# The state-space mixer of a two-layer transformer kernel: wave rows kept as three rows, all state products on GpSimd, deeper weight prefetch

## The chip, the cores and the metric

The kernel runs on one core of one Trainium2 chip, as one program. The metric is the device time of one execution in microseconds. The kernel before was run three times: median 3163.51 us, from 3159.57 to 3173.73. One further execution was recorded by the hardware profiler.

A core has engines that run side by side, each through its own list of instructions in order: TensorE (PE; its weight loads are listed apart as PEld), VectorE (DVE), ScalarE (ACT), GpSimd (POOL) and SyncE (SP, which here only issues transfers). They wait for one another through semaphores. A transfer is issued by SP, ScalarE or GpSimd into that engine's queue, and the transfers of one queue are issued in the order of the engine's list.

## The reference, cut to what matters

The model has two layers over 1024 latent tokens and 256 context tokens of width 1024. Layer 0 mixes tokens by attention and retention, layer 1 by a state-space mixer; each is followed by an MLP. The change lies in the mixer of layer 1:

```python
def s5_scan(u, a_bar, b_bar, c_mat, x0):      # complex, diagonal, 64 groups of 16 channels, 64 states each
        bu = jnp.einsum('btgh,gph->btgp', u_blk, b_bar)
        bu = bu.at[:, 0].add(a_bar * x)
        _, xs = lax.associative_scan(_affine_compose, (a, bu), axis=1)   # x_t = a_bar * x_{t-1} + bu_t
        y = jnp.einsum('btgp,ghp->btgh', xs, c_mat).real
...
    y_cf, x_cf = s5_scan(u_c, ab_f, bb_f, c_f, x0)                 # context first, forward
    y_cb, x_cb = s5_scan(u_c[:, ::-1], ab_b, bb_b, c_b, x0)        # and backward
    y_lf, _ = s5_scan(u_l, ab_f, bb_f, c_f, x_cf)
    y_lb, _ = s5_scan(u_l[:, ::-1], ab_b, bb_b, c_b, x_cb)
    y = y_lf + y_lb[:, ::-1] + d_skip * u
    z = gelu(y) @ w_glu;  out = z[:, :D] * sigmoid(z[:, D:])
```

## The kernel before, in words

**The mixer stage** is `s5_main`. The sequence is cut into chunks of 8 tokens: 160 columns, 32 of context and 128 of latents. Per group the chunk's inputs are multiplied into 64 complex states, the states are scanned over the 160 chunks, and the outputs come from the states plus a direct term inside the chunk (the matrix `T`). The complex decay is a real decay times a rotation. The rotation is taken out of the scan: the chunk inputs are multiplied by cosine and sine waves (rotated back), then a real scan runs, then the scanned states are rotated forward again by the same waves. So each step with a wave is four real products, and needs cosine, sine and negated sine.

The 64 groups are handled as 32 **pairs** `q` (two groups of 64 states fill the 128 partitions). For one pair:

- `load(q)`: SP issues the transfers of the pair's weights: `B` and `C` (256 KB each), the wave rows `CS` (320 KB, two rows from DRAM into rows 2 and 3 of a tile of four, three such tiles in rotation) and `T` in two parts. The loop calls it three pairs ahead.
- `spread(q)`, on ScalarE, called one pair ahead: L1493 writes the negated sine into row 0 of `CS`, L1494 copies the cosine into row 1, and L1497 writes the two decay rows `dec` of the scan (two `dec` tiles in rotation).
- `states(q)`: TensorE makes the chunk inputs (L1510) into two PSUM banks `b`, one per direction. VectorE multiplies each by the wave rows (L1516, `st`, twice: one 128x640 instruction per direction), adds the two halves (L1519, `sm`) and scans both directions in one instruction (L1521, `sz`). The forward rotation is one product per direction (L1527, `sy`, `e` in the code): on GpSimd, or on VectorE where `(2q+d) % 3` is zero, which is one product in two of every three pairs.
- `outs(q)`, called two pairs later: TensorE adds the direct term (L1539) and the states' outputs (L1545, 32 matmuls) into two banks `z` and `b` that stay open over four pairs; then four GELUs on ScalarE (L1550) write them to two of the 16 tiles `y`.

The inputs are read as `ut`, eight chunk positions by 16 channels on partitions. They are written to DRAM (`ud`) by the normalization that precedes the stage (`s5_in`: L1457 makes `us` on ScalarE, L1461 stores it) and read back by `inputs()`, L1472, eight transfers for eight groups, the first eight divided between ScalarE's and SP's queues.

**What sets the order.** The loop gives the program order and with it priorities; a tile scheduler orders each engine's instructions by these priorities and by what is ready in its own estimate. An engine then runs its list strictly in order. Buffers come from rotating pools: weights `B` and `C`, products `sy`, outputs `y` and many tiles of the stages around share 32 buffers of 128x512 (`atile`), and taking one waits until its former user is done. The 16 `y` tiles are taken when the stage starts.

**What follows** is the gated linear stage `glu`: it transposes `y` (L1586) and splits it into a high and a low part (`yh`, `yl`; L84). A side generator (`ada_rest`) computes modulation vectors for the last MLP: GpSimd issues broadcasts of a vector (`silr`, L201) and loads of weights (`aw`, L215), VectorE multiplies and reduces each (L219, called `ISA` in the order, `CUSTOM_DVE_ANT_0` in the trace). The scheduler mixes this work into the end of the mixer stage.

## Time and profile before

| | before |
|---|---|
| median of 3 runs | 3163.51 us (3159.57 to 3173.73) |
| profiled execution | 3176.57 us |
| its span, first to last instruction | 3174.8 us |
| mean granted TensorE clock | 0.965 of full speed |
| busy share of the span: PE, DVE, ACT, POOL | 93, 68, 39, 27 % |
| mixer stage, roughly | 2070 to 2240 us |
| busy in these 170 us: PE, DVE, ACT, POOL | 137.89, 147.46, 62.29, 70.39 us |

Times in the rows are microseconds unless marked ns. A row of the timeline has the start, the length, the engine, the line, the operation, the tile names as out<-in with the shape, the count, and in brackets the idle time just before it with what ended it. A row of the groups has the line, engine, operation and shapes, the count, then the busy time in all and the mean of one in ns, then the idle time of the engine just before these instructions and what ended most of it. A row of the windows has the stretch, its length, the busy time and count of PE, PEld, DVE, ACT and POOL, the granted clock, the busy share of the transfer engines and GB/s.

### The profile page before, as it was taken

To read this page: it belongs to the slowest core of one execution; us is meant where nothing else is said; L and a number is where in the kernel's file an instruction comes from. 1 tells how busy PE (TensorE), PEld (TensorE's weight loads), DVE (VectorE), ACT (ScalarE), POOL (GpSimd) and SP (SyncE) were. 2 spreads that over 40 slices of the span, in tenths; PEclk is the share of its full clock that TensorE was granted. 3 is DMA by queue.
4 is the path that set the end of the run, shared out by engine and by line. 5 is a ranking of instruction groups with operands and counts; after the bars stand their busy time and mean duration, and the time that the engine had idled before them with its cause. 6 is when DMAs were issued, how large, how long until landed. Compare 5 with 4: busy or idle time off the path is not lost. (4 is left out here: it accounts for less than half of the span.)

```text
span 3174.8 us, 45240 instructions
## 1 busy us (share of the span) xinstructions
PE 2967.9 (93%) x16683; PEld 2447.3 (77%) x16683; DVE 2143.4 (68%) x4088; ACT 1247.0 (39%) x2543; POOL 867.7 (27%) x936
## 2 busy tenths in 40 slices
PE   5899998899999999999998899878799999999998
PEld 3777777778878788888887777767578788888887
DVE  7776777777764588466676997488845555556555
ACT  6543322567672322333243367434234322222221
POOL 3642222355450131111113313133722111111111
PEclk8999998899999999999999999989899999999999
DMA  8132222210003252233329856498632111111111
GB/s 253 63 126 76 82 80 69 70 41 25 14 21 120 78 174 90 62 103 102 96 85 236 247 172 185 120 196 233 223 101 87 54 46 47 54 47 53 43 45 67
DMA packets 223774, 324.32 MB, mean 102 GB/s; under 512 B 52432, under 2 KB 147440, under 8 KB 223552
## 3 DMA queue, kind: packets, MB, share of 16 engines
q1 hardware_dynamic: 143376, 234.48, 25.0%
q0 software_dynamic: 20336, 49.70, 5.7%
q10 hardware_dynamic: 59840, 37.24, 3.9%
q8 instruction: 131, 2.15, 0.3%
q14 instruction: 91, 0.75, 0.1%
HBM read 267.96 MB, written 53.36 MB: 101 GB/s over the span
## 5 line engine op out<-in xcount | busy, mean ns | idle before, releaser
L84 POOL TENSOR_TENSOR al<-r,ah 128x512 fp32r<-128x512 f32 (+1 forms) x160 | 210.6, 1329 | 1258.2 <-ACT r L1064 1159.8
L1077 DVE SCALAR_TENSOR_TENSOR x<-b,mods,x 128x512 f32<-128x512 f32 (+1 forms) x483 | 460.5, 967 | 106.6 <-PE b L72 100.0
L84 DVE TENSOR_TENSOR ul<-mraw,uh 128x512 fp32r<-128x512 f32 x256 | 195.8, 770 | 387.3 <-ACT uh L76 386.7
L70 PE MATMUL b<-ah,dh 128*128 128x512 f32 (+1 forms) x1088 | 412.7, 380 | 3.5 <-ACT r L1060 1.5
L71 PE MATMUL b<-al,dh 128*128 128x512 f32 (+1 forms) x1088 | 411.1, 378 | 0.7 <-POOL al L84 0.7
L72 PE MATMUL b<-ah,dl 128*128 128x512 f32 (+1 forms) x1088 | 410.3, 378 | 0.0
L76 ACT ACTIVATE uh<-mraw 128x512 fp32r<-128x512 f32 x256 | 160.3, 628 | 466.9 <-PE b L71 255.9
L70 PE MATMUL b<-h2h,uh 128*128 128x512 f32 (+1 forms) x768 | 280.5, 365 | 28.2 <-DVE x L1077 22.1
L72 PE MATMUL b<-h2h,ul 128*128 128x512 f32 (+1 forms) x768 | 277.7, 362 | 6.2 <-DVE ul L84 6.2
L71 PE MATMUL b<-h2l,uh 128*128 128x512 f32 (+1 forms) x768 | 276.8, 360 | 0.0
L70 PEld LDWEIGHTS b<-ah,dh 128*128 128x128 f32 x1088 | 205.3, 189 | 42.7 <-issue 2.3
L72 PEld LDWEIGHTS b<-ah,dl 128*128 128x128 f32 x1088 | 205.3, 189 | 38.3
L71 PEld LDWEIGHTS b<-al,dh 128*128 128x128 f32 x1088 | 205.4, 189 | 38.2 <-POOL al L84 1.1
L76 ACT ACTIVATE dh<-mraw 128x512 fp32r<-128x512 f32 x192 | 116.0, 625 | 225.3 <-PE b L71 95.8
L70 PE MATMUL b<-h3h,uh 128*128 128x512 f32 x512 | 202.3, 396 | 0.0
L71 PE MATMUL b<-h3l,uh 128*128 128x512 f32 x512 | 200.1, 391 | 2.0 <-DVE h3l L316 1.8
L72 PE MATMUL b<-h3h,ul 128*128 128x512 f32 x512 | 201.2, 394 | 0.0
L84 POOL TENSOR_TENSOR pl<-pe,ph 128x512 fp32r<-128x512 f32 (+1 forms) x128 | 158.9, 1249 | 153.2 <-ACT ph L76 81.7
L70 PEld LDWEIGHTS b<-h2h,uh 128*128 128x128 f32 x768 | 146.3, 190 | 57.2 <-DVE x L1077 26.3
L1060 ACT ACTIVATE r<-b 128x512 f32<-128x512 f32 (+1 forms) x160 | 88.1, 551 | 239.6 <-PE b L72 184.9
L70 PE MATMUL z<-wh,hh 128*128 128x512 f32 (+1 forms) x400 | 161.1, 403 | 12.2 <-ACT scr L500 6.8
L72 PEld LDWEIGHTS b<-h2h,ul 128*128 128x128 f32 x768 | 146.7, 191 | 31.3 <-DVE ul L84 7.4
(426 smaller groups left out, 7195.0 us busy)
## 6 DMA issues: line engine op xcount, KB each, us to landing
mraw<-in_w SPq DMA_DIRECT2D x192, 512.0 KB
aw<-in_adat SPq DMA_DIRECT2D x64, 256.0 KB
mraw<-in_glu SPq DMA_DIRECT2D x32, 512.0 KB
aw<-in_adat POOLq DMA_DIRECT2D x48, 256.0 KB, 5.2
aw<-in_adat POOLq DMA_DIRECT2D x96, 128.0 KB, 3.6
CS<-csd SPq DMA_DIRECT2D x32, 320.0 KB
w<-in_adaw SPq DMA_DIRECT2D x32, 256.0 KB
wraw<-in_winr SPq DMA_DIRECT2D x32, 256.0 KB
```

The costliest lines, as they stand in the source:

```text
L70: mm(o, s[0], m[0], start=start, stop=False)
L71: mm(o, s[0], m[1], start=False, stop=False)
L72: mm(o, s[1], m[0], start=False, stop=stop)
L76: self.nc.scalar.activation(o, x, AF.Copy)
L84: e.tensor_tensor(o, x, h.bitcast(F32), ALU.subtract)
L1060: nc.scalar.activation(r[:, :n], b[:, :n], AF.Relu)
L1077: nc.vector.scalar_tensor_tensor(o, as_x(b), self.M[:, l, 5, oc, s:s + 1], xs, op0=ALU.mult, op1=ALU.add)
```

## The change

The wave tile holds three rows instead of four: sine and cosine come from DRAM (the two rows of `csd` swap places), and ScalarE writes only the negated sine behind them, one instruction per pair instead of two. The products read the three rows as two overlapping pairs: `turned` builds an access pattern that starts at the cosine row and steps one row up for one half of the result and one row down for the other. The wave tiles rotate over four instead of three and have their own loader `load_waves`, four pairs ahead. All products `sy` go to GpSimd. `B`, `C` and `T` are fetched up to six pairs ahead, fewer as the `y` tiles fill up, since a `y` tile is now taken when its four pairs are done. Of the stores of `us` for the last block of tokens, those of odd tiles move from SP's queue to GpSimd's, and the first eight loads of `ut` are divided between GpSimd and SP instead of ScalarE and SP.

```diff
@@ -1337,8 +1337,8 @@
                 nc.scalar.activation(t2(l), t2(l), AF.Sin, scale=-2.0 * math.pi, bias=self.hpi)
 
                 def store():
-                    nc.scalar.dma_start(self.csd[:, g0:g0 + n, 1], t3(q))
-                    nc.scalar.dma_start(self.csd[:, g0:g0 + n, 0], t3(l))
+                    nc.scalar.dma_start(self.csd[:, g0:g0 + n, 0], t3(q))
+                    nc.scalar.dma_start(self.csd[:, g0:g0 + n, 1], t3(l))
                 self.later(1, store)
             self.later(2, waves)
             yield
@@ -1458,7 +1458,7 @@
                                  AF.Identity, bias=sh)
             rows = self.ud[kt * P:(kt + 1) * P]
             for c0 in ((32 + t0 // 8,) if t0 < NL else (0, 160)):
-                (nc.sync if bi == 1 else nc.gpsimd).dma_start(rows[:, :, c0:c0 + nchunk], us.rearrange("p (s c) -> p s c", s=8))
+                (nc.sync if bi == 1 and kt % 2 == 0 else nc.gpsimd).dma_start(rows[:, :, c0:c0 + nchunk], us.rearrange("p (s c) -> p s c", s=8))
         return self.norm(1, 0, 1 if t0 >= NL else 0, lambda kt: x[:, kt, t0:t0 + n], n, o, tmp, b)
 
     def s5_main(self, p, last):
@@ -1471,27 +1471,36 @@
             for s in range(8):
                 engs[s % len(engs)].dma_start(ut[112 - 16 * s:128 - 16 * s, g0:g0 + n],
                                   self.ud[16 * g0:16 * (g0 + n), s].rearrange("(g q) c -> q g c", q=16))
-        self.Y = {(kt, th): self.atile(name="y") for kt in range(KT) for th in range(2)}
-        sl, A, ybank, decs = {}, {}, {}, {}
+        self.Y = {}
+        sl, A, ybank, decs, waves = {}, {}, {}, {}, {}
+
+        def load_waves(q):
+            waves[q] = p.tile([P, 2, 3, 160], F32, tag="CS", name="CS", bufs=4)
+            nc.sync.dma_start(waves[q][:, :, 0:2], self.csd[:, 2 * q:2 * q + 2])
 
         def load(q):
             B, C = (self.atile(name=nm).rearrange("p (d w k) -> p d w k", d=2, w=2) for nm in "BC")
             nc.sync.dma_start(B, self.bst[:, q])
-            CS = p.tile([P, 2, 4, 160], F32, tag="CS", name="CS", bufs=3)
-            nc.sync.dma_start(CS[:, :, 2:4], self.csd[:, 2 * q:2 * q + 2])
             nc.sync.dma_start(C, self.cst[:, q])
             Tt = self.atile(256, F32, "T").rearrange("p (k n) -> p k n", k=2)
             for k in range(2):
                 nc.sync.dma_start(Tt[:, k], bass.AP(
                     tensor=self.tst.tensor, offset=self.tst.offset + (2 * q + k) * 7680,
                     ap=[[16, 8], [240, 16], [1, P]]))
-            sl[q] = B, C, Tt, CS
+            sl[q] = B, C, Tt
+
+        def turned(CS, d, up, c):
+
+            a = CS[:, d, 1, c].unsqueeze(1).unsqueeze(1).to_broadcast([P, 2, 2, c.stop - c.start])
+            row = CS.ap[2][0]
+            ap = [list(x) for x in a.ap]
+            ap[1][0], ap[2][0] = (-row, row) if up else (row, -row)
+            return bass.AP(tensor=a.tensor, offset=a.offset, ap=ap)
 
         def spread(q):
 
-            CS = sl[q][3]
-            nc.scalar.activation(CS[:, :, 0], CS[:, :, 3], AF.Copy, scale=-1.0)
-            nc.scalar.activation(CS[:, :, 1], CS[:, :, 2], AF.Copy)
+            CS = waves[q]
+            nc.scalar.activation(CS[:, :, 2], CS[:, :, 0], AF.Copy, scale=-1.0)
             dec = p.tile([P, 2, 2, 160], F32, tag="dec", name="dec", bufs=2)
             for d in range(2):
                 nc.scalar.activation(dec[:, d], mask, AF.Copy, scale=self.R8[:, 2 * q + d:2 * q + d + 1])
@@ -1499,7 +1508,7 @@
 
         def states(q):
 
-            B, C, Tt, CS = sl[q]
+            B, CS = sl[q][0], waves[q]
             dec = decs.pop(q)
             t = p.tile([P, 2, 2, 320], F32, tag="st", name="st", bufs=1)
             for d in range(2):
@@ -1512,25 +1521,23 @@
                 vv = vb[:, 0:320].rearrange("p (r c) -> p r c", r=2)
                 if d == 1:
                     vv = vv[:, :, ::-1]
-                cs = CS[:, d].rearrange("p (r w) c -> p r w c", r=2)
                 v.tensor_tensor(t[:, d].rearrange("p r (w c) -> p r w c", w=2),
-                                vv.unsqueeze(2).to_broadcast([P, 2, 2, 160]), cs[:, ::-1], ALU.mult)
+                                vv.unsqueeze(2).to_broadcast([P, 2, 2, 160]), turned(CS, d, False, slice(0, 160)),
+                                ALU.mult)
             sm = p.tile([P, 2, 320], F32, tag="sm", name="sm", bufs=1)
             v.tensor_tensor(sm, t[:, :, 0], t[:, :, 1], ALU.add)
             z = p.tile([P, 2, 2, 160], F32, tag="sz", name="sz", bufs=2)
             v.tensor_tensor_scan(z.rearrange("p d r c -> p (d r c)"), dec.rearrange("p d r c -> p (d r c)"),
                                  sm.rearrange("p d c -> p (d c)"), 0.0, ALU.mult, ALU.add)
             for d in range(2):
-                cs = CS[:, d].rearrange("p (r w) c -> p r w c", r=2)
                 y = self.atile(name="sy").rearrange("p (r w c) -> p r w c", r=2, w=2)
-                e = gp if (2 * q + d) % 3 else v
-                e.tensor_tensor(y if d == 0 else y[:, :, :, ::-1],
-                                z[:, d, :, 31:159].unsqueeze(2).to_broadcast([P, 2, 2, P]), cs[:, :, ::-1, 31:159],
+                gp.tensor_tensor(y if d == 0 else y[:, :, :, ::-1],
+                                z[:, d, :, 31:159].unsqueeze(2).to_broadcast([P, 2, 2, P]), turned(CS, d, True, slice(31, 159)),
                                 ALU.mult)
                 A[q, d] = y
 
         def outs(q):
-            B, C, Tt, CS = sl[q]
+            B, C, Tt = sl[q]
 
             if q % 4 == 0:
                 ybank[0], ybank[1] = self.bank("z"), self.bank()
@@ -1545,12 +1552,18 @@
                         mm(o[k][H], A[q, d][R, r, w, H], C[R, d, w], start=False, stop=d == 1 and r == 1 and w == 1)
             if q % 4 == 3:
                 for th in range(2):
+                    self.Y[q // 4, th] = self.atile(name="y")
                     yo = self.Y[q // 4, th].rearrange("p (t j k h) -> p k j t h", t=4, k=2, h=16)
                     for k in range(2):
                         nc.scalar.activation(yo[:, k], ybank[k].rearrange("p (j t h) -> p j t h", j=4, h=16)[
                             :, :, 4 * th:4 * th + 4], self.gelu)
 
-        for q in range(3):
+
+        ahead = lambda q: min(6, 11 - (q + 2) // 4)
+        for q in range(4):
+            load(q)
+            load_waves(q)
+        for q in range(4, 6):
             load(q)
         ut = p.tile([P, 64, 192], F32, name="ut")
         mask = p.tile([P, 2, 160], F32, name="mask")
@@ -1558,7 +1571,7 @@
         v.memset(mask[:, :, 0:1], 0.0)
         for _ in range(3):
             next(last)
-        inputs(0, 8, (nc.scalar, nc.sync))
+        inputs(0, 8, (nc.gpsimd, nc.sync))
         self.drain(last)
         spread(0)
         for q in range(32):
@@ -1567,8 +1580,10 @@
                 spread(q + 1)
             if q % 4 == 0 and q < 28:
                 inputs(2 * q + 8, 8)
-            if q < 29:
-                load(q + 3)
+            while len(sl) < min(32, q + 1 + ahead(q)):
+                load(len(sl))
+            if q < 28:
+                load_waves(q + 4)
             if q > 1:
                 outs(q - 2)
         outs(30)
```

What this does to the engines' lists is shown at four places.

VectorE's list in the middle of the stage (one pair is two `st`, `sm`, the scan `sz`). Before:

```order
L1521 SCALAR_TENSOR_TENSOR sz<-dec,sm 128x640
L1527 TENSOR_TENSOR sy<-sz,CS 128x4x128
L1516 TENSOR_TENSOR st<-b,CS 128x640 x2
L1519 TENSOR_TENSOR sm<-st 128x640
L1521 SCALAR_TENSOR_TENSOR sz<-dec,sm 128x640
```

After:

```order
L1530 SCALAR_TENSOR_TENSOR sz<-dec,sm 128x640
L1524 TENSOR_TENSOR st<-b,CS 128x640 x2
L1528 TENSOR_TENSOR sm<-st 128x640
L1530 SCALAR_TENSOR_TENSOR sz<-dec,sm 128x640
```

The product `sy` that stood behind the scan is gone from VectorE in every pair; two stand on GpSimd for each pair.

ScalarE's list around the second group of four GELUs. Before (the `dec` rows and the two wave rows of one pair, then the GELUs of pairs 4 to 7, then the next pairs):

```order
L1497 ACTIVATE dec<-mask,R_12289 128x320 x5
L1493 ACTIVATE CS<-CS 128x2x160
L1494 ACTIVATE CS<-CS 128x2x160
L1550 ACTIVATE y<-z 128x4x4x16
L1550 ACTIVATE y<-b 128x4x4x16
L1550 ACTIVATE y<-z 128x4x4x16
L1550 ACTIVATE y<-b 128x4x4x16
L1493 ACTIVATE CS<-CS 128x2x160
L1494 ACTIVATE CS<-CS 128x2x160
L1497 ACTIVATE dec<-mask,R_12289 128x320
```

After:

```order
L1506 ACTIVATE dec<-mask,R_12289 128x320 x6
L1558 ACTIVATE y<-z 128x4x4x16
L1558 ACTIVATE y<-b 128x4x4x16
L1558 ACTIVATE y<-z 128x4x4x16
L1558 ACTIVATE y<-b 128x4x4x16
L1503 ACTIVATE CS<-CS 128x2x160 x3
L1506 ACTIVATE dec<-mask,R_12289 128x320 x2
```

Before, one pair's two wave rows stand between the last decay row and the GELUs, and those of the next pair right behind them, ahead of a single further decay row. After, the decay rows run on through one pair more, the GELUs follow, and the negated row of each of the next three pairs stands behind them.

VectorE's list at the end of the stage, where the reductions (L219) come in. Before, from the scan of pair 29:

```order
L1521 SCALAR_TENSOR_TENSOR sz<-dec,sm 128x640
L1516 TENSOR_TENSOR st<-b,CS 128x640 x2
L219 ISA aw,mods<-aw,silr_22772,adab 128x256
L219 ISA mods 128x1
L1519 TENSOR_TENSOR sm<-st 128x640
L219 ISA aw,mods<-aw,silr_22774,mods 128x256
```

After, from the `st` of pair 29:

```order
L1524 TENSOR_TENSOR st<-b,CS 128x640 x2
L1528 TENSOR_TENSOR sm<-st 128x640
L219 ISA aw,mods<-aw,silr_22740,adab 128x256
L219 ISA mods 128x1
L1530 SCALAR_TENSOR_TENSOR sz<-dec,sm 128x640
L219 ISA aw,mods<-aw,silr_22742,mods 128x256
```

The first reduction stands ahead of the scan of pair 29, where it stood inside pair 30. In all 15 reductions instead of 7 stand ahead of the last scan.

GpSimd's list at the same place. Before:

```order
L1527 TENSOR_TENSOR sy<-sz,CS 128x512
L1527 TENSOR_TENSOR sy<-sz,CS 128x4x128
L215 DMA aw<-in_adat 128x256 x11
L1527 TENSOR_TENSOR sy<-sz,CS 128x4x128
L215 DMA aw<-in_adat 128x256 x6
L1527 TENSOR_TENSOR sy<-sz,CS 128x512
L215 DMA aw<-in_adat 128x256 x42
```

After:

```order
L1534 TENSOR_TENSOR sy<-sz,CS 128x512
L1534 TENSOR_TENSOR sy<-sz,CS 128x4x128
L201 DMA silr_22746<-scd 128x256
L215 DMA aw<-in_adat 128x256 x9
```

Then, in this order, two products, nine loads, two products, seven loads, two products and 42 loads. The first loads of `aw` now stand behind the products of pair 28 instead of 29, and one of the four `silr` broadcasts behind them too.

SP's list at the start of the stage. Before:

```order
L1461 DMA ud<-us 1024x1x64 x3
L1472 DMA ut<-ud 16x8x192 x4
L1461 DMA ud<-us 1024x1x64 x5
```

After:

```order
L1461 DMA ud<-us 1024x1x64 x3
L1472 DMA ut<-ud 16x8x192 x4
L1461 DMA ud<-us 1024x1x64
```

The three stores ahead of the first loads are those of tiles 0, 1 and 2 before, and of tiles 0, 2 and 4 after. GpSimd's list now holds two stores, the other four loads of `ut` and two more stores.

## The prediction

> **What bounds the kernel now.** I read the page first, to see where the change can matter, then the windows, the groups and the timeline of one stage. The page says that TensorE carries most of the span:
>
> ```profile
> span 3174.8 us, 45240 instructions
> PE 2967.9 (93%) x16683; PEld 2447.3 (77%) x16683; DVE 2143.4 (68%) x4088; ACT 1247.0 (39%) x2543; POOL 867.7 (27%) x936
> ```
>
> But everything that the change touches lies in one stage, the state-space mixer between the two MLPs, and there another engine sets the pace. First the window of that stage (columns: length, busy time of PE, PEld, DVE, ACT, POOL, clock, DMA share, GB/s), then its groups on VectorE and GpSimd:
>
> ```profile
> 2070.00:2240.00 170.00, 137.89 (x2617) 116.97 (x2615) 147.46 (x166) 62.29 (x147) 70.39 (x64) 0.89 0.87 213
> ...
> L1516 DVE TENSOR_TENSOR st<-b,CS 128x640 f32<-128x640 f32 x64 | 49.7, 814 | 24.0 <-ACT CS L1494 11.7 <-issue 10.0 <-PE b L1510 2.3
> L1521 DVE TENSOR_TENSOR_SCAN sz<-dec,sm 128x640 f32<-128x640 f32 x32 | 47.7, 1491 | 3.0
> L1519 DVE TENSOR_TENSOR sm<-st 128x640 f32<-128x640 f32 x32 | 33.0, 1030 | 1.0
> L1527 DVE TENSOR_TENSOR sy<-sz,CS 128x512 f32<-128x512 f32 x22 | 17.9, 815 | 0.3
> L1527 POOL TENSOR_TENSOR sy<-sz,CS 128x512 f32<-128x512 f32 x42 | 59.1, 1418 | 116.9 <-DVE sz L1521 81.2 <-issue 11.6 <-DMA T<-tst 7.0
> ```
>
> VectorE is busy 147 of 170 us. The 32 sums `sm` take 33.0 us, 6.6 more than 32 times the 0.825 of most of them: six took about 1.1 us longer. Each pair ends in its scan, so I measure the stage by the distance from scan to scan. The timeline of VectorE, with GpSimd's rows beside it, shows the two kinds of interval that matter here:
>
> ```profile
> 2072.84 1.49 DVE L1521 TENSOR_TENSOR_SCAN sz<-dec,sm 128x640 f32<-128x640 f32 x1
> ...
> 2078.01 1.49 DVE L1521 TENSOR_TENSOR_SCAN sz<-dec,sm 128x640 f32<-128x640 f32 x1
> 2080.99 0.83 DVE L1519 TENSOR_TENSOR sm<-st 128x640 f32<-128x640 f32 x1
> 2081.95 1.49 DVE L1521 TENSOR_TENSOR_SCAN sz<-dec,sm 128x640 f32<-128x640 f32 x1
> ...
> 2158.45 1.49 DVE L1521 TENSOR_TENSOR_SCAN sz<-dec,sm 128x640 f32<-128x640 f32 x1
> 2159.86 1.53 DVE L1516 TENSOR_TENSOR st<-b,CS 128x640 f32<-128x640 f32 x2
> 2161.43 1.95 DVE L1519 TENSOR_TENSOR sm<-st 128x640 f32<-128x640 f32 x1
> 2163.51 1.49 DVE L1521 TENSOR_TENSOR_SCAN sz<-dec,sm 128x640 f32<-128x640 f32 x1
> ...
> 2216.46 1.49 DVE L1521 TENSOR_TENSOR_SCAN sz<-dec,sm 128x640 f32<-128x640 f32 x1
> ...
> 2236.96 1.48 DVE L1521 TENSOR_TENSOR_SCAN sz<-dec,sm 128x640 f32<-128x640 f32 x1
> 2079.64 1.29 POOL L1527 TENSOR_TENSOR sy<-sz,CS 128x512 f32<-128x512 f32 x1 [3.80 <-DVE sz L1521]
> 2160.18 2.52 POOL L1527 TENSOR_TENSOR sy<-sz,CS 128x512 f32<-128x512 f32 x2 [2.99 <-DVE sz L1521]
> ```
>
> With one product on GpSimd (2079.64 to 2080.93) the sum `sm` starts after it, takes 0.83 us, and the next scan comes after 3.94 us. With both products there (2160.18 to 2162.70) the same sum starts at 2161.43, lasts 1.95 us and ends at 2163.38, 0.68 us after GpSimd is done: it was held. The next scan comes after 5.06 us. The scans of pair 0 and pair 28 are 143.62 us apart, 5.13 us per pair.
>
> **The steady interval.** All products on GpSimd make every pair a pair of the second kind. The 0.69 us product leaves VectorE in two pairs of three, and in its place the sum waits. I price a plain interval at 5.05 us. The lower bound is 3.94, if the sum were not held.
>
> The Trainium skill ("SBUF — State Buffer", section "SBUF: two separate sides") says that VectorE with two SBUF inputs and GpSimd take a shared port by an exclusive lock, whole instruction by whole instruction, whoever starts first. The held sum of 1.95 us agrees; but instruction by instruction the sum could also slip in between GpSimd's two products, which the same row does not show, and that is the second case below.
>
> **The wave rows on ScalarE.** The multiplications `st` of a pair need the negated wave row, which ScalarE writes in program order behind the decay rows `dec`, and the `dec` of pair q+2 wait for the scan of pair q. ScalarE and VectorE around pair 16, then pair 12, and the table load of the first GELU:
>
> ```profile
> 2165.03 1.01 ACT L1497 ACTIVATE dec<-mask,R 128x320 f32<-128x320 f32 x2 [3.98 <-DVE sz L1521]
> 2165.95 0.45 ACT L1493 ACTIVATE CS<-CS 128x320 f32<-128x320 f32 x1
> 2166.31 0.45 ACT L1494 ACTIVATE CS<-CS 128x320 f32<-128x320 f32 x1
> 2166.67 0.36 ACT L1550 ACTIVATE y<-z 128x256 f32<-128x256 f32 x1
> 2166.80 1.55 DVE L1516 TENSOR_TENSOR st<-b,CS 128x640 f32<-128x640 f32 x2 [1.80 <-ACT CS L1494]
> 2167.47 0.39 ACT L1550 ACTIVATE y<-b 128x256 f32<-128x256 f32 x1
> ...
> 2146.64 1.56 DVE L1516 TENSOR_TENSOR st<-b,CS 128x640 f32<-128x640 f32 x2 [1.74 <-ACT CS L1494]
> 2149.16 1.49 DVE L1521 TENSOR_TENSOR_SCAN sz<-dec,sm 128x640 f32<-128x640 f32 x1
> 2105.30 1.28 ACT L1550 ACT_TABLE_LOAD   x1
> ```
>
> Once in four pairs the wave is late already: 1.80 us here, 11.7 us in all by the group of L1516. The prefetch does not cure it, because the wait is for ScalarE's order and not for a transfer. The listing of the change puts two more things ahead of that wave: the `dec` rows run one pair further ahead, so that both `dec` of pair q+1 (waiting for the scan of q-1) and all four GELUs stand before the wave of pair q. From the end of the scan: two `dec` 0.92 us (2165.03 to 2165.95), four GELUs 0.27 each (2166.67 to 2167.47 is three of them), 1.07, one wave row 0.47, in all 2.5 us before `st` starts. From `st` to the next scan is 2.52 us when nothing holds the sum (2146.64 to 2149.16; by then GpSimd is done), and the scan's own 1.49 makes 6.51 us. This hits pairs 12, 16, 20, 24 and 28; pair 8 also has the 1.28 us table load, which now no longer hides behind `st`: 7.79. In front of pair 4 there are two `dec` and a wave, no GELU: 1.4+2.52+1.49, about 5.45. One negated row fewer (0.36) is already in this.
>
> Pairs 0 to 28: 21 plain intervals 106.1, one 5.45, one 7.79, five of 6.51 are 32.6: **151.9 us against 143.6, 8.3 us more**. Without the late waves it would be 28 times 5.05, 141.4, 2.2 us less.
>
> **The prefetch.** It can take away only what VectorE waits for transfers: 2.3 us behind PE (group of L1516) and part of ScalarE's lateness. My intervals hold no such wait, so the whole of it is credited. Late output buffers issue nothing; they only make room for the weights. The swapped wave rows change no count.
>
> **The end of the stage.** There the generator of the next stage mixes in modulation work: GpSimd issues the `aw` loads, VectorE reduces them.
>
> ```profile
> 2222.83 2.54 POOL L1527 TENSOR_TENSOR sy<-sz,CS 128x512 f32<-128x512 f32 x2 [0.82 <-issue]
> 2225.31 5.88 POOL L215 DMA_DIRECT2D aw<-in_adat  x11
> 2228.12 0.48 DVE L219 CUSTOM_DVE_ANT_0 aw<-aw,silr,adab 128x256 f32<-128x256 f32 x1 [4.07 <-DMA aw<-in_adat]
> 2273.02 2.20 DVE L219 CUSTOM_DVE_ANT_0 aw<-aw,silr,mods 128x256 f32<-128x256 f32 x1
> 2255.89 0.69 DVE L84 TENSOR_TENSOR yl<-b,yh 128x512 fp32r<-128x512 f32 x1
> 2256.63 2.31 PE L1586 MATMUL b<-ident,y 128*128 128x128 f32 x8 [9.69 <-DVE yl L84]
> ```
>
> Before, 7 reductions stand ahead of the last scan; in the change 15, the first one already ahead of the scan of pair 29. Counted from the end of the scan of pair 28: products done at 2.7, a table load of `silr` 0.55, first `aw` issued at 3.25, landed 2.8 later (2225.31 to 2228.12) at 6.1, reduction 0.41, scan 29 at 6.5: interval 8.0. Nine issues of 0.54 keep GpSimd until about 8.1, its two products until 10.7. Eight reductions (3.3), `st` 1.53 and `sm` 0.82 then stand before scan 30: 7.2 us of interval if nothing holds them, 10.1 if the reductions wait for GpSimd, as the 2.20 us one did at 2273.02 where 0.48 is usual. Scan 30 to 31 in the same way: 6.3 or 7.8. Sum 21.5 to 26.0 against 20.50 (2216.46 to 2236.96), so 1.0 to 5.5 more; I take 5.5, since the products are the same kind of work as what held 2273.02. From the last scan to `yl`, which releases PE, stand 26 reductions before and after: 0.5 for the second product on GpSimd.
>
> **The start.** The first matmuls wait for `ut`:
>
> ```profile
> 2055.69 2.11 ACT L1457 ACTIVATE us<-u,mods 128x512 f32<-128x512 f32 x2
> 2056.88 2.79 SPq L1461 DMA_DIRECT2D ud<-us  x3
> 2060.11 3.18 SPq L1472 DMA_DIRECT2D ut<-ud  x4
> 2068.67 6.30 PE L1510 MATMUL b<-ut,B 128*64 128x160 f32 x48 [13.95 <-DMA ut<-ud]
> 2060.00:2070.00 10.00, 1.33 (x10) 1.21 (x12) 0.12 (x1) 4.38 (x5) 0.00 (x0) 0.50 1.15 170
> ```
>
> SP's three stores ahead of `ut` are now those of tiles 0, 2 and 4; the fifth `us` ends at 2060.7 (0.96 apart), its store is issued by 2061.6: 1.5 us later than 2060.11. Two more stores of 256 KB go out ahead, on GpSimd's queue, 1.5 us each at 170 GB/s. Between 0 and 4.6, if all of it counts; I take 2, since the other half of `ut` no longer stands behind SP.
>
> **Sum:** 8.3+5.5+0.5+2 = 16.3 us more on the profiled execution of 3176.57 us. That execution ran 13 us above the median of the runs, 3163.51, and the added waits do not depend on that, so the forecast for the median is **3179.5 us**. Half a percent, about what a measurement of this kernel can tell from no change, is 15.8 us.
>
> **Rivals.**
> - *The sum slips in.* If VectorE gets its turn between GpSimd's two products, plain intervals fall to 3.94: 21 of them 82.7, the rest 45.8, 128.5 in all, 15.1 less; end 1.0 and start 2 more: 12 less, **3151**. For it: a lock taken per instruction. Against it: the 1.95 us of the row above and the five others that the group's 6.6 us hold; none of the six slipped in.
> - *The waves are not late.* ScalarE keeps up, the lock stays: 2.2 less, 8 more at start and end: **3169**.
> - *The change does what it says.* The sum slips in and ScalarE keeps up too: 28 times 3.94 is 110.3, 33.3 less, 3 more: **3133**, faster. It decides from the point at which `sm` stays at 0.83 with both products there and `st` starts with the end of the scan at pair 12. Against it stands ScalarE's order.
> - *Transfers are the bound.* They fill 0.87 of the 170 us, 148 us, so a longer stage has room for them unless they bunch: one more wait for `ut` like the 13.95 us of PE's row at the start, behind the weights that now go six pairs ahead on SP's queue, makes 3179.5 into **3193**.
>
> **How the numbers follow.** Forecast 0.72 (its own range, from its end and start bounds, 3170 to 3187, is half beyond the 15.8), sum slips in 0.10, waves not late 0.06, works as meant 0.05, transfers 0.07. Slower: 0.40 of the forecast and the transfers, 0.47. Faster: 0.05 and a little of the slip, 0.07. Same: 0.46. The range leaves out the fast case and some of each neighbour: 3156 to 3193.
>
> **What would show it.** Plain scan-to-scan intervals near 5.05 and `sm` near 1.9 in nearly all pairs; `st` waiting 2.5 us for ScalarE at pairs 8, 12, 16, 20, 24, 28; 151.9 us from scan 0 to 28 and 24 to 26 from there to 31; first matmul 2 us later. It is wrong if `sm` stays at 0.83, if `st` never waits for the wave, or if PE or transfers end the waits ahead of `st`.

## The result, and the profile after

The changed kernel took 3183.11 us in the median of eight runs (3179.86 to 3196.86), the kernel before 3165.01 us beside it: a ratio of 1.0050, with a 95% interval from 1.0034 to 1.0067. By the ratio that is some 16 us more, 11 to 21 by the interval; the two medians themselves lie 18.1 apart. The forecast was 16 more.

The spans of the two profiled executions differ by 6.8 us only, because differences outside the stage hide part of it: the one of before, 3176.57 us, lies 11.6 above the median of its eight runs, and it enters the stage 4.68 us later. In the profiles of the experiments below, the time from the stage's end to the last instruction scatters by 6 us in no order that follows the edits, so I take these differences as chance. The stage is therefore measured from a landmark that the change does not touch, the last `rsc` of the normalization (L238), to the first `yl` after the stage. The timelines of both, first before:

```profile
2052.74 0.26 ACT L238 ACTIVATE rsc<-b,eps 128x4 f32<-128x4 f32 x1 [1.70 <-PE b L235]
```

After, with the first matmul, two scans of the steady part and GpSimd's work between them, and the end of the stage:

```profile
2048.06 0.26 ACT L238 ACTIVATE rsc<-b,eps 128x4 f32<-128x4 f32 x1 [2.88 <-PE b L235]
2068.55 0.80 PE L1519 MATMUL b<-ut,B 128*64 128x160 f32 x4 [17.89 <-DMA ut<-ud]
2072.71 1.49 DVE L1530 TENSOR_TENSOR_SCAN sz<-dec,sm 128x640 f32<-128x640 f32 x1
...
2077.53 1.49 DVE L1530 TENSOR_TENSOR_SCAN sz<-dec,sm 128x640 f32<-128x640 f32 x1
2079.10 2.54 POOL L1534 TENSOR_TENSOR sy<-sz,CS 128x512 f32<-128x512 f32 x2 [2.29 <-DVE sz L1530]
2080.50 1.82 DVE L1528 TENSOR_TENSOR sm<-st 128x640 f32<-128x640 f32 x1
2082.46 1.49 DVE L1530 TENSOR_TENSOR_SCAN sz<-dec,sm 128x640 f32<-128x640 f32 x1
...
2223.99 1.49 DVE L1530 TENSOR_TENSOR_SCAN sz<-dec,sm 128x640 f32<-128x640 f32 x1
...
2249.97 1.48 DVE L1530 TENSOR_TENSOR_SCAN sz<-dec,sm 128x640 f32<-128x640 f32 x1
...
2266.42 0.69 DVE L84 TENSOR_TENSOR yl<-b,yh 128x512 fp32r<-128x512 f32 x1
```

From these rows and those of before, in us:

| | before | after | difference |
|---|---|---|---|
| `rsc` to the first matmul | 15.93 | 20.49 | +4.56 |
| `rsc` to scan 0 | 20.10 | 24.65 | +4.55 |
| scan 0 to scan 28 | 143.62 | 151.28 | +7.66 |
| scan 28 to scan 31 | 20.50 | 25.98 | +5.48 |
| scan 31 to the first `yl` | 18.93 | 16.45 | -2.48 |
| `rsc` to the first `yl` | 203.15 | 218.36 | +15.21 |

The groups of VectorE in the changed stage (2070 to 2250 us) say why:

```profile
L1528 DVE TENSOR_TENSOR sm<-st 128x640 f32<-128x640 f32 x32 | 50.6, 1580 | 1.0
L1524 DVE TENSOR_TENSOR st<-b,CS 128x640 f32<-128x640 f32 x64 | 49.3, 811 | 32.1 <-ACT CS L1503 18.0 <-issue 13.9 <-PE b L1519 0.2
L1530 DVE TENSOR_TENSOR_SCAN sz<-dec,sm 128x640 f32<-128x640 f32 x32 | 47.7, 1491 | 3.2
```

VectorE lost its products, 17.9 us in the group of before, and got 17.6 of it back in the sums: 50.6 us against 33.0, the same 32 instructions on the same sizes. The wait of `st` for the wave row rose from 11.7 to 18.0 us; the wait for TensorE's banks, the one a deeper prefetch could shorten, fell from 2.3 to 0.2. A late wave, before pair 12:

```profile
2130.91 1.49 DVE L1530 TENSOR_TENSOR_SCAN sz<-dec,sm 128x640 f32<-128x640 f32 x1
2132.44 1.01 ACT L1506 ACTIVATE dec<-mask,R 128x320 f32<-128x320 f32 x2 [3.99 <-DVE sz L1530]
...
2134.15 0.39 ACT L1558 ACTIVATE y<-b 128x256 f32<-128x256 f32 x1
2134.41 1.20 ACT L1503 ACTIVATE CS<-CS 128x320 f32<-128x320 f32 x3
2134.93 1.55 DVE L1524 TENSOR_TENSOR st<-b,CS 128x640 f32<-128x640 f32 x2 [2.52 <-ACT CS L1503]
2136.52 0.82 DVE L1528 TENSOR_TENSOR sm<-st 128x640 f32<-128x640 f32 x1
```

The decay rows wait for the scan, then come the GELUs, then the wave, then `st`, 2.52 us late. By then GpSimd is done, and the sum takes 0.82.

### The profile page after: what moved, and what is told of

The parts are those of the page before. It is cut to its first block, busy times and chain, and to the rows that moved or that the text cites. A ratio compares the mean times of both kernels' runs of the same rounds, so it can differ in the third digit from the quotient of the medians.

```text
span 3181.6 us, 45210 instructions
## 1 busy us (share of the span) xinstructions
PE 2970.8 (93%) x16683; PEld 2444.6 (77%) x16683; DVE 2150.6 (68%) x4066; ACT 1232.9 (39%) x2511; POOL 898.1 (28%) x966
## 5 line engine op out<-in xcount | busy, mean ns | idle before, releaser
L70 PEld LDWEIGHTS b<-h2h,uh 128*128 128x128 f32 x768 | 146.5, 191 | 50.6 <-DVE x L1077 19.8
```

The costliest lines, as they stand in the source:

```text
L70: mm(o, s[0], m[0], start=start, stop=False)
```

## The experiments

My theory had three parts: the sum is held while GpSimd works; the deeper prefetch moves the lists of ScalarE and, at the end, of VectorE so that waves and scans come late; and the start waits for stores and loads that were moved. Each run below undoes one part or does one alone. All distances are read as in the table above, each from one profiled execution, and a ratio is to the kernel before on the same chip.

| run | to first matmul | scan 0 to 28 | 28 to 31 | `rsc` to `yl` | median us | ratio (95%) |
|---|---|---|---|---|---|---|
| before | 15.93 | 143.62 | 20.50 | 203.15 | | 1 |
| changed | 20.49 | 151.28 | 25.98 | 218.36 | 3183.11 | 1.0050 (1.0034 to 1.0067) |
| changed, products divided again | 20.78 | 146.73 | 24.69 | 212.24 | 3169.72 | 1.0017 (1.0003 to 1.0031) |
| before, all products on GpSimd | 16.42 | 146.54 | 22.67 | 209.63 | 3171.32 | 1.0027 (1.0006 to 1.0048) |
| changed, prefetch of three | 20.57 | 139.38 | 21.97 | 203.44 | 3161.42 | 0.9998 (0.9982 to 1.0014) |
| changed, start undone | 15.90 | 151.39 | 25.79 | 213.77 | 3175.40 | 1.0029 (1.0012 to 1.0045) |
| changed, only the loads of the start undone | 17.74 | 151.41 | 25.54 | 215.38 | 3174.82 | 1.0027 (1.0011 to 1.0043) |
| prefetch and start undone | 16.44 | 139.56 | 21.97 | 198.66 | 3160.01 | 0.9991 (0.9967 to 1.0015) |
| the same, products divided | 15.71 | 136.75 | 20.53 | 193.60 | 3157.59 | 0.9984 (0.9960 to 1.0009) |
| changed, sum from PSUM | 20.67 | 134.29 | 23.79 | 199.56 | 3157.59 | 0.9983 (0.9961 to 1.0006) |
| prefetch and start undone, sum from PSUM | 16.45 | 125.90 | 21.55 | 185.73 | 3147.57 | 0.9966 (0.9944 to 0.9989) |
| the same, `ut` two loads per pair | 16.47 | 139.08 | 21.84 | 197.44 | 3162.55 | 0.9988 (0.9971 to 1.0006) |
| before, sum from PSUM | 16.43 | 146.50 | 21.09 | 206.76 | 3167.82 | 1.0007 (0.9990 to 1.0024) |

How far one execution can be trusted shows in kernels whose edits leave a stretch alone. From scan 0 to 28, the changed kernel and the two with the start undone lie within 0.13 us, and the two with a prefetch of three and products undivided within 0.18. The first matmul comes between 15.71 and 16.47 us in the eight kernels with the start of before, and between 20.49 and 20.78 in the four with the changed start.

### The products alone

```diff
-                e = gp if (2 * q + d) % 3 else v
+                e = gp
```

> The kernel before with one part of the change alone: all products on GpSimd. Four wave rows, prefetch of three pairs, early output buffers and the start are as before; ScalarE's list keeps one pair's wave rows ahead of the GELUs. Theory (held sum): 22 plain intervals of 5.05 and six of about 5.75 (the wave 1.8 us late, the sum then not held), 145.5 us from scan 0 to 28 against 143.6 before; 2 and then 9 reductions stand ahead of the scans of pairs 30 and 31, so 1 to 3.5 us more at the end; in all 3 to 5 us more, about 3169. Rival (the change does what it says, the sum slips in): plain intervals of 3.94, the time falls by 20 or more. Rival (nothing held, only the load of VectorE moved): sums of 0.83 us in all pairs.

The stage took 146.54 us from scan 0 to 28, and 22.67 to scan 31; the ratio 1.0027 is clear of 1. This is the theory's answer, not that of a change that does what it says: the sums took 48.8 us. VectorE was relieved of 22 products and the stage became longer.

In two intervals, though, a sum was not held. VectorE and GpSimd around one of them, in this kernel:

```profile
2143.31 1.49 DVE L1521 TENSOR_TENSOR_SCAN sz<-dec,sm 128x640 f32<-128x640 f32 x1
2145.03 3.21 POOL L1527 TENSOR_TENSOR sy<-sz,CS 128x512 f32<-128x512 f32 x2 [3.37 <-DMA C<-cst]
2146.28 0.83 DVE L1519 TENSOR_TENSOR sm<-st 128x640 f32<-128x640 f32 x1
2147.21 2.38 DVE L1521 TENSOR_TENSOR_SCAN sz<-dec,sm 128x640 f32<-128x640 f32 x1
...
2153.16 1.49 DVE L1521 TENSOR_TENSOR_SCAN sz<-dec,sm 128x640 f32<-128x640 f32 x1
```

GpSimd started 1.72 us behind the start of the scan (1.57 in the row of after above), so its first product ended at about 2146.3 (half of 2.53 behind 2145.03), when the sum was ready, and the sum ran then. GpSimd's two products took 3.21 us instead of 2.53, and now the scan was held: 2.38 us instead of 1.49. The intervals are 3.90 and 5.95, together 9.85, where two plain ones make 10.1. The other place gives 9.82, and two such places in the run with the start undone (below) give 10.03 and 9.87. So a sum that slips in gains next to nothing; the wait goes to the scan behind it. In the row of after the sum is ready at 2080.50, and GpSimd's second product began at about 2080.37: it missed the turn by 0.1 us.

The reverse, the changed kernel with the products divided again:

```diff
-                gp.tensor_tensor(y if d == 0 else y[:, :, :, ::-1],
+                (gp if (2 * q + d) % 3 else v).tensor_tensor(y if d == 0 else y[:, :, :, ::-1],
```

> The changed kernel with one part undone: the products are divided again between VectorE and GpSimd as in the kernel before (a product with (2q+d) % 3 == 0 on VectorE); three wave rows, prefetch, late output buffers and the start stay changed. Theory (the sum is held while GpSimd works): pairs with one product on GpSimd come at 3.94 + 0.69 = 4.63 us from scan to scan, pairs with both at 5.05; nine or ten of the 28 intervals from scan 0 to 28 have both, so 9.3 x 5.05 + 18.7 x 4.63 = 133.6 plus some 10 us of late wave rows, 144 us against 151.3 with the change; the time falls by about 7 to 3176 us. Rival (the products on GpSimd cost nothing, VectorE's own load counts): 19 products of 0.69 us return to VectorE and the time rises by up to 13 to 3196.

It became faster, as the theory has it: 4.55 us from scan 0 to 28 (7 were expected) and 6.1 over the whole stage. The ratio fell by 0.0033, some 10 us, of which the stage shows 6; the intervals of the two ratios leave room for that. The sums took 34.0 us, and `st` still waited 14.7 us for the wave rows.

### The sum from PSUM

If the sum is held because both of its inputs are in SBUF, one input elsewhere must free it. Each `st` is split by the component of the input; the second half is written over its own PSUM bank, and the sum reads it there:

```diff
-                v.tensor_tensor(t[:, d].rearrange("p r (w c) -> p r w c", w=2),
-                                vv.unsqueeze(2).to_broadcast([P, 2, 2, 160]), turned(CS, d, False, slice(0, 160)),
-                                ALU.mult)
+                w4 = turned(CS, d, False, slice(0, 160))
+                o1 = vb[:, 0:320].rearrange("p (w c) -> p w c", w=2)
+                if d == 1:
+                    o1 = o1[:, :, ::-1]
+                u1.append(o1)
+                for r, o in ((0, t[:, d].rearrange("p (w c) -> p w c", w=2)), (1, o1)):
+                    v.tensor_tensor(o, vv[:, r].unsqueeze(1).to_broadcast([P, 2, 160]), w4[:, r], ALU.mult)
...
-            v.tensor_tensor(sm, t[:, :, 0], t[:, :, 1], ALU.add)
+            for d in range(2):
+                v.tensor_tensor(sm[:, d].rearrange("p (w c) -> p w c", w=2), t[:, d].rearrange("p (w c) -> p w c", w=2), u1[d], ALU.add)
```

> The changed kernel, with the sum sm reading one of its two inputs from PSUM: each st is split in two of 320 columns, the half of the imaginary part is written over its own PSUM bank, and sm is split in two, one per direction (three more VectorE instructions per pair, 0.1 us each). Theory (the sum is held because both its inputs are in SBUF while GpSimd works there): the sums start and end at once, 0.43 us each, beside GpSimd's products; plain intervals fall from 5.05 to between 4.1 (GpSimd's 2.6 and the scan's 1.41) and 4.5 (the transfers of a pair, 0.87 x 5.13); the late intervals stay at 6.5 since the wave rows are still late. 21 plain intervals save 12 to 20 us: about 3166. Rival (GpSimd's memory traffic slows or orders the sum whatever its inputs): sums still end only after GpSimd's products, intervals of 5.05 plus 0.3 for the three instructions, about 3190.

The plain intervals fell from 5.05 to 4.30, and 17 us went from scan 0 to 28, inside the 12 to 20 expected. The late intervals stayed, at 6.34.

The same where no wave is late. First the kernel to compare with, prefetch and start undone together (their edits stand below):

> The changed kernel with two parts undone, the six-pair prefetch and the start; all products on GpSimd, three wave rows loaded four pairs ahead and late output buffers stay. Theory: the two gains add, first matmul 16 us behind rsc, 139.4 us from scan 0 to 28, about 22 to scan 31; about 3156. Rival (they hide one another: an earlier start only waits longer for the transfers of the first pairs): 3161, as with the prefetch undone alone.

It kept 139.56 us from scan 0 to 28 and 57.4 us of sums. In the stage the two gains add, 198.66 us against 203.44 with the prefetch alone undone; the timing (3160 against 3161) cannot tell them apart. Then the PSUM edit on it:

> The kernel of the run before (prefetch and start undone) with the sum reading one input from PSUM. Theory (held sum): with no wave late, all 28 intervals fall from 4.98 to between 4.1 and 4.5, 115 to 126 us from scan 0 to 28; about 3133 to 3144, below the kernel before. Rival (a resource beside the sum binds at about 5 us per pair: TensorE, transfers): intervals stay near 5 and waits for PE or for transfers appear ahead of st; about 3156.

VectorE and GpSimd in that kernel:

```profile
2135.65 2.53 POOL L1540 TENSOR_TENSOR sy<-sz,CS 128x512 f32<-128x512 f32 x2 [1.69 <-PE b L1558]
2136.81 0.48 DVE L1534 TENSOR_TENSOR sm<-st,b 128x320 f32<-128x320 f32 x1
2137.20 0.49 DVE L1531 TENSOR_TENSOR b<-b,CS 128x320 f32<-128x320 f32 x1
2137.73 0.49 DVE L1534 TENSOR_TENSOR sm<-st,b 128x320 f32<-128x320 f32 x1
2138.35 1.49 DVE L1536 TENSOR_TENSOR_SCAN sz<-dec,sm 128x640 f32<-128x640 f32 x1
```

GpSimd works from 2135.65 to 2138.18. Both sums start meanwhile and take 0.48 and 0.49 us; nothing is held. This kernel is faster than the one before, 0.9966 of its time (0.9944 to 0.9989), and its stage is 12.9 us shorter than that of the run above. Only this edit differs from the run above it, so the 13.7 us between scan 0 and 28 are what the held sum cost, less the three added instructions. A sum split in two with both inputs in SBUF was not run; but the halves here run beside GpSimd's products and not between them, so their shortness alone does not explain it. The 125.90 us lie at the slow end of what was expected, and the rival is there in part: three intervals of 5.4 to 6.5 us, in which `st` waits for TensorE. In the two longest, 6.49 and 5.99, TensorE waits 2.73 and 2.29 us for `B`, which stands behind eight `ut` loads on SP's queue; in the third its wait of 2.20 us is put down to VectorE's scan. The window shows the transfers (columns as before):

```profile
2080.00:2200.00 120.00, 103.92 (x2168) 88.12 (x2167) 108.48 (x189) 45.92 (x104) 68.57 (x54) 0.97 0.94 242
```

The PSUM edit on the kernel before, with the products still divided:

> The kernel before with the sum reading one input from PSUM, as in the two runs with that edit, and nothing else changed (products divided between VectorE and GpSimd, four wave rows, prefetch of three). Theory (the held sum costs only where both products of a pair are on GpSimd; otherwise VectorE's own work binds): six sums save 1.1 us, and each of 32 pairs pays 0.3 for three more instructions: 9.6 - 6.6, so 3 us more, 3166. The edit pays only together with the products on GpSimd, where it saved 13.7 us from scan 0 to 28. Rival (the split sum is faster in any setting, for instance because PSUM is read faster): 10 or more us less here too.

2.9 us more from scan 0 to 28, as worked out. The edit is no gain in itself; it pays only where the sum is held.

### The prefetch

```diff
-        ahead = lambda q: min(6, 11 - (q + 2) // 4)
-        for q in range(4):
-            load(q)
-            load_waves(q)
-        for q in range(4, 6):
-            load(q)
+        ahead = lambda q: 3
+        for q in range(4):
+            if q < 3:
+                load(q)
+            load_waves(q)
```

> The changed kernel with the weights B, C and T fetched three pairs ahead again instead of up to six; the wave rows stay four ahead, everything else stays changed. In the engines' lists this puts the decay rows back to one pair less ahead of the GELUs, and 0, 2 and 9 reductions ahead of the last three scans instead of 1, 9 and 15. Theory (the loss at the GELUs and at the end is the order that the deeper prefetch makes): no st waits for ScalarE by more than a few tenths at pairs 8, 12, 16, 20, 24, 28, so 28 x 5.05 = 141.4 us from scan 0 to 28 instead of 151.3, and 21 to 23 us from there to scan 31 instead of 26.0; the time falls by 13 to 15 to about 3169. Rival (the prefetch saves waits for transfers, the order hardly matters): st and the matmuls wait for transfers instead, and the time stays at 3183 or rises.

The groups of VectorE in that kernel's stage:

```profile
L1528 DVE TENSOR_TENSOR sm<-st 128x640 f32<-128x640 f32 x32 | 57.2, 1789 | 1.0
L1524 DVE TENSOR_TENSOR st<-b,CS 128x640 f32<-128x640 f32 x64 | 49.1, 807 | 14.2 <-issue 14.0 <-PE b L1519 0.2
```

No `st` waits for ScalarE any more, 18.0 us before the edit, and none waits for transfers either, though the weights come only three pairs ahead. The stage became 14.9 us shorter and the ratio went from 1.0050 to 0.9998. All sums but three are held (57.2 us), and every interval is within 4.82 to 5.08: this is the pure pace of held sums. ScalarE's list around the second group of GELUs:

```order
L1506 ACTIVATE dec<-mask,R_12289 128x320 x4
L1558 ACTIVATE y<-z 128x4x4x16
L1558 ACTIVATE y<-b 128x4x4x16
L1558 ACTIVATE y<-z 128x4x4x16
L1558 ACTIVATE y<-b 128x4x4x16
L1503 ACTIVATE CS<-CS 128x2x160 x2
```

Four decay rows stand ahead of the GELUs instead of six. The last two now wait for the scan one pair earlier, and decay rows, GELUs and wave are done while that pair is still at work.

### The start

The stores and the first loads as before:

```diff
-                (nc.sync if bi == 1 and kt % 2 == 0 else nc.gpsimd).dma_start(rows[:, :, c0:c0 + nchunk], us.rearrange("p (s c) -> p s c", s=8))
+                (nc.sync if bi == 1 else nc.gpsimd).dma_start(rows[:, :, c0:c0 + nchunk], us.rearrange("p (s c) -> p s c", s=8))
...
-        inputs(0, 8, (nc.gpsimd, nc.sync))
+        inputs(0, 8, (nc.scalar, nc.sync))
```

> The changed kernel with the start undone: all eight stores of us on SP's queue and the first eight loads of ut divided between ScalarE and SP, as before; everything else stays changed. Theory (the first matmul waits for the later store and the shared transfers): the first matmul comes about 16 us after the norm's rsc instead of 20.5, and the time falls by 4.5 to 3178.5. Rival (the start is hidden behind something else, or the difference of 4.6 was chance in the two profiles): the first matmul stays at 20 us behind rsc, or it comes earlier and the time stays at 3183.

The first matmul came 15.90 us behind `rsc`, 4.6 earlier, and the stage became 4.6 shorter. With the loads alone undone:

> The changed kernel with half of the start undone: the first eight ut loads go to ScalarE's and SP's queues again, while the stores of odd tiles stay on GpSimd's. It divides the 4.6 us of the start: if the later store on SP (tile 4 instead of 2 ahead of the loads) costs it, SP's four loads still start 1.7 us late and the first matmul comes 17.6 to 18 us behind rsc; if GpSimd's loads and their landing (6.6 us) cost it, it comes at 16; if the stores that share the transfers cost it, it stays near 20.5. Time between 3175 and 3183, not resolved by the timing alone.

It came after 17.74 us. So some 2.75 of the 4.6 us belong to the four loads on GpSimd's queue and some 1.84 to the stores, as the store of tile 4 ahead of SP's loads had it; the scatter of 0.8 us among kernels with the start of before goes into both figures. The timing (1.0029 and 1.0027) cannot tell these two kernels apart.

### Two that did not come as expected

The products divided again, where prefetch and start are undone:

> The kernel with prefetch and start undone and the products divided between VectorE and GpSimd as before; three wave rows loaded four pairs ahead and late output buffers stay. Theory (held sum): intervals of 4.63 where one product is on GpSimd and 5.05 where both are, 133.6 us from scan 0 to 28 against 139.4 with all on GpSimd; about 3150. Rival (with ScalarE on time GpSimd takes the products at no cost): VectorE's 0.69 us come on top in two of three pairs and the time rises to 3162 or more.

136.75 us from scan 0 to 28, 2.8 less and not 5.8: `st` waited for the wave row at two places (4.3 us in its group), since this division changes ScalarE's list once more. The direction is the theory's, and the timing cannot tell the two kernels apart.

The fastest kernel with `ut` loaded in twos:

```diff
-            if q % 4 == 0 and q < 28:
-                inputs(2 * q + 8, 8)
+            m, k = divmod(q + 6, 4)
+            if 1 < m < 8:
+                inputs(8 * m, 8, part=range(2 * k, 2 * k + 2))
+            if q == 0:
+                inputs(8, 8)
```

> The fastest kernel so far (sum with one input from PSUM, prefetch and start undone) with one more edit: the eight ut loads of a block of four pairs are no longer issued together but two per pair, up to two pairs earlier. Theory (the long intervals of 5.4 to 6.5 us in that kernel are matmuls that wait for weights B behind eight ut loads, 7 us of SP's queue, with transfer engines 0.94 busy): these waits of 5 us in all between scans 0 and 28 vanish, 28 x 4.32 = 121 us instead of 125.9; about 3143. Rival (the transfers themselves bind at 0.94, not their bunching): the same bytes take the same time, waits for B spread over other pairs, and the time stays at 3147.

Both the theory and its rival failed: 139.08 us, 13 more. Between scans 0 and 28, `st` waits for TensorE at 14 places, 17.1 us in all, against three places and 4.5 us before the edit; that is the 13. The waits for `B` did not vanish: TensorE waits for it seven times, 8.5 us in all (9.3 before the edit), and `st` waits behind each, 7.1 us together. So the waits spread over other pairs as the rival had it, but the time did not stay. The longest interval up to scan 28, 9.61 us, shows a cause of another kind, TensorE's own order:

```profile
2115.38 0.80 PE L1552 MATMUL z<-T,ut 128*128 128x128 f32 x2 [3.80 <-ACT y L1564]
2118.53 0.49 DVE L1531 TENSOR_TENSOR st<-b,CS 128x320 f32<-128x320 f32 x1 [5.13 <-PE b L1520]
```

TensorE stands at the first output matmul of the next four pairs, which waits for the GELUs to free the bank `z`, and the chunk inputs that `st` needs are queued behind it. This happens twice and costs `st` 6.3 of the 17.1 us. The 3.7 us at the five remaining places, and whether the bunched loads would have been the bound in another order, stay open.

## Why the prediction was right

The sum came to 16.3 us, the stage measures 15.2, and the timing 16. The two terms that carry the forecast held: 13.8 us were forecast for the late waves, the held sums and the reductions up to the last scan, and 13.1 were measured. That the whole came as close is luck: the start cost 2.6 us more than its term, and the stretch behind the last scan 3.0 less. (The forecast of 3179.5 also lies 0.3 below what 16.3 on 3163.51 gives.) Step by step:

- **The steady interval** held: 22 of the 32 sums take 1.81 to 1.97 us, and plain intervals 4.82 to 5.08 (5.05 was taken). "Nearly all pairs" was too much: the sums of the six late pairs, of pair 4, of the first pair and of the last two are not held. The PSUM run shows the cause: with one input of the sum in PSUM nothing is held. The rule that the prediction took from the Trainium skill ("SBUF — State Buffer", section "SBUF: two separate sides"), a lock for whole instructions in the order of arrival, agrees with these rows (the sum at 2080.50 in the profile after takes 1.82 us, a sum alone 0.83), and the slip shows the same for the scan (2.38 us against 1.49).
- **The wave rows** held to two tenths: 2.52 us late (2.5), late intervals of 6.53 (6.51), pair 4 at 5.45 (5.45), pair 8 at 7.96 (7.79); 151.28 from scan 0 to 28 (151.9). But the prediction read this from the lists without naming what made the order, and it priced the prefetch only by the waits for transfers that it could remove. The run with three pairs shows that the prefetch is what moved ScalarE's list. It is the largest single part of the loss, 14.9 us of the stage.
- **What the wave rows gain** was missing. "The swapped wave rows change no count" is true, yet three rows loaded four pairs ahead let ScalarE keep up once the prefetch is three: from the kernel before with all products on GpSimd to the one with prefetch and start undone the stage falls from 209.63 to 198.66. In one chain from before to after: products +6.5, wave rows and late output buffers together -11.0, start +4.8, prefetch +14.9; that is +15.2. The wave rows and the output buffers were not tried apart.
- **The end of the stage** came to 25.98 us (26.0), with other parts: 8.76, 9.18 and 8.04 for 8.0, 10.1 and 7.8, so the equal sum is luck. The first `aw` landed 3.6 us behind its issue and not 2.8, and two of the eight reductions before scan 30 were held, not all. From the last scan to `yl` the prediction added 0.5, and 2.48 were saved. Its count of reductions was right, but before, VectorE had waited 4.14 us there for a load of `aw`, and its last product had taken 1.75 us; after, with the loads issued earlier, 0.8 us of waits for loads and two reductions of 1.5 us are left.
- **The start** was mis-sized. The bounds were 0 and 4.6, the value taken 2, "since the other half of `ut` no longer stands behind SP". That reason failed: the half on GpSimd's queue is what costs 2.75 us, and the upper bound was the answer.
- **The rival in which the sum slips in** was priced wrongly. It happened, twice in each of two runs, and gained 0.07 to 0.28 us over two intervals, where 1.1 for each was assumed. GpSimd's two products, the sum and the scan need about 2.53+0.83+1.49 = 4.85 us one after the other, whichever goes first, so 3.94 was not to be had pair after pair with both products on GpSimd and both inputs of the sum in SBUF.

## What to carry to other kernels

Before work is moved from VectorE to GpSimd, add up what takes turns: here two products, the sum and the scan, about 4.85 us per pair, against 3.94 for the interval that VectorE alone would need. An operand that can stay in PSUM takes an instruction out of that sum; here it was worth 0.75 us per plain interval. With prefetch and start undone, moving the products alone made the stage longer (198.66 us against 193.60 divided), and together with the sum from PSUM it came to 185.73; the timing does not separate this last kernel from the divided one (0.9966 and 0.9984, intervals overlapping). And a prefetch that is deeper than any wait for transfers requires is not free under a scheduler that orders by its own estimate: read what it does to the lists of the other engines, above all to short instructions that someone waits for.

## What was not expected of the hardware

A held instruction is shown as a long one: the sum reads 1.82 us in the trace and 0.83 alone, the scan 2.38 and 1.49, so a longer mean in a group can be a wait that no column names. In the profile after, a tenth of a microsecond decided the turn (the sum ready at 2080.50, GpSimd's second product begun at about 2080.37). The reductions of the next stage took turns in the same way, two of them beside GpSimd's two products in the changed kernel:

```profile
2243.49 2.85 POOL L1534 TENSOR_TENSOR sy<-sz,CS 128x512 f32<-128x512 f32 x2 [0.66 <-DVE sz L1530]
2243.72 1.49 DVE L219 CUSTOM_DVE_ANT_0 aw<-aw,silr,adab 128x256 f32<-128x256 f32 x1
2245.14 1.49 DVE L219 CUSTOM_DVE_ANT_0 aw<-aw,silr,mods 128x256 f32<-128x256 f32 x1
2246.56 0.47 DVE L219 CUSTOM_DVE_ANT_0 aw<-aw,silr,mods 128x256 f32<-128x256 f32 x1
```

Each was held for 1.0 us, and GpSimd's two products took 2.85 us instead of 2.53. VectorE's own last product in the kernel before was held as well:

```profile
2238.52 1.43 POOL L1527 TENSOR_TENSOR sy<-sz,CS 128x512 f32<-128x512 f32 x1 [0.66 <-DVE sz L1521]
2238.74 1.75 DVE L1527 TENSOR_TENSOR sy<-sz,CS 128x512 f32<-128x512 f32 x1
...
2248.82 0.48 DVE L219 CUSTOM_DVE_ANT_0 aw<-aw,silr,adab 128x256 f32<-128x256 f32 x1 [4.14 <-DMA aw<-in_adat]
```

It took 1.75 us where 0.69 is usual; the last row is the wait of 4.14 us named above.
